# Strassen's scheme for the recurrence's values, and the token sums made earlier in the program, in a one-core hybrid decoder layer

## The chip, the cores and the metric

The kernel runs on one core of one Trainium2 chip. A core has a matmul engine (TensorE, PE in the profile, with its weight loads as PEld), an elementwise engine (VectorE, DVE), an activation engine (ScalarE, ACT), a general engine (GpSimd, POOL), a queue engine (SyncE, SP), and 16 DMA engines that serve the queues of SP, ACT and POOL. The metric is the device time of one execution in microseconds (us), as the median of several runs.

## What is computed

A decoder layer on x of 512 tokens by 1024 channels, float32. After an RMS norm, h goes through one wide matrix `w_in`; its columns are split into the inputs of two branches and of their gates. The first branch is a gated linear recurrence with 8 heads of 128 channels, the second a latent attention. What matters here is the first branch:

```
proj = h @ w_in[l]
hq, hf, hi, hz, cq, ckv, kr, mz, glog = split(proj)
f = lb + (1 - lb) * sigmoid(hf);  q = silu(hq);  k = 1 - f;  v = hi
o = hgrn2_recurrence(q, k, v, log(f))           # S_t = diag(f_t) S_{t-1} + k_t v_t^T,  o_t = S_t^T q_t
y_a = rms_norm(o, hg_norm_g) * silu(hz)
y_b = mla_branch(cq, ckv, kr, mz, ...)
gates = sigmoid(glog + b_gate)
x = x + (gates_a * (y_a @ w_proj_a) + gates_b * (y_b @ w_proj_b)) @ w_out
out = rms_norm(x, final_norm_g)
```

The values v are hi = h @ w_in[:, 2048:3072]: 512 x 1024 times 1024 x 1024.

## The kernel before

**Precision.** Every float32 matmul is made of three. Each operand is split into a high part (rounded to the matmul's format by ACT) and a low part (what is left, by DVE), and high x high, high x low and low x high are added up in PSUM. `mm3` (L99) issues the three for one k (a block of 128 channels). `load_w` (L110) fetches a weight piece of 128 x 1024 elements by SP's queue into one of three raw buffers, casts its high part on ACT (L129) and subtracts for the low part on DVE (L130); there are four buffers for high and four for low parts. `split` (L169) does the same for data that is in SBUF or PSUM already.

**Stages.** First x is normed and transposed into hT, which holds h as channels by tokens, high and low (to about 25 us). Then the latent projection (L398 to L403), its norms, and the transposes into cT (L425). Then the recurrence by pairs of heads, `hg_pair` (L585): the forget projection, `hg_forget` (the gates' running products on DVE and POOL), then for pairs 0 and 2 the values of four heads at once, the query projection, transposes, states, the gate projection, scores and outputs. For pairs 1 and 3 the gate projection stands where the values are. Then the attention heads, and last the two gates' projections, the two output projections and `w_out`.

**The values.** `proj_tok` (L151) makes 512 columns for all 512 tokens: two rounds of two token tiles of 128, eight k each, three matmuls of 128 x 512 each, 96 in all. Its four weight pieces stay in their buffers until the second round has used them. ACT copies each tile to SBUF (`v_sb`, L603). Pair 0 makes the columns of heads 0 to 3, pair 2 those of heads 4 to 7.

**Strassen's scheme elsewhere.** The gates' projections, `w_proj_a` and `w_out` are done already as seven products of half blocks instead of eight, in Winograd's form. They need four sums of blocks of h (s1 to s4) and four sums of blocks of the weight. The weight sums are made in DRAM: SP copies a block (`BlockSums.start`, one copy queued behind each weight load, L793), and POOL's queue adds another block by an accumulating DMA (`BlockSums.add`, L800). `step` (L845) issues one such sum at fixed places in the pairs and heads, from the list `adds`, behind the last POOL instruction traced. The sums of h are made by `early_sums` (L816) in two halves, one inside pair 0 and one behind it, and SP writes their high and low parts to DRAM (L830), from where POOL's queue fetches them before the gates (L1002).

**What orders the work.** Some blocks are marked as scheduled by hand for PE, ACT or DVE. Everything else is ordered before the run by the framework, engine by engine, from a model of durations: of the instructions that it holds for ready, the one traced first goes first. `tc.issue_after(x)` puts instructions behind x on x's engine. On the chip every engine takes its instructions in that fixed order and waits by semaphores; a queue's DMAs are issued in order too. A pool of tiles with one buffer per tag makes a new tile wait for the last reader of the old one.

Of the kernel before, what the change touches and what calls it, by code (L numbers as in the profile page):

```python
# [9 lines left out]
F32 = mybir.dt.float32  # L10
# [28 lines left out]
def hybrid_layer(ctx: ExitStack, tc: tile.TileContext, a):  # L39
# [67 lines left out]
    last_hi, last_lo = [None], [None]  # L107
    queued = []

    def load_w(*pieces, to=None):  # L110
# [4 lines left out]
        for src in pieces:  # L115
# [12 lines left out]
            o += n  # L128
        last_hi[0] = nc.scalar.copy(hi[:, :o], raw[:, :o])  # L129
# [51 lines left out]
    kpe = Pair(cpool.tile([P, 2, S], F32R, "kpe")[:])  # L181
    cw = Pool("cwork", "right")
# [23 lines left out]
    x_sb = [st.tile([P, D], F32, "x", bufs=NT) for _ in range(NT)]  # L206
# [50 lines left out]
    def squares(t):  # L257
        sq = st.tile([P, D], F32, "sq", bufs=2)
        nc.scalar.activation(sq[:], x_sb[t][:], AF.Square, accum_out=rss[t][:, 0:1])
        power(rss[t][:, 0:1], rss[t][:, 0:1], 1.0 / D, EPS, neg_half[:, 0:1])  # L260
# [17 lines left out]
    def c_product(t, kh, kind, ks=range(4)):  # L278
# [3 lines left out]
        for k in ks:  # L282
            nc.tensor.matmul(ps, hT[l][:, 4 * kh + k, t * P : t * P + P], c_hl[kh][r][:, k * 256 : k * 256 + 256],  # L283
                             start=kh == 0 and kind == 0 and k == 0, stop=kh == 1 and kind == FIN and k == 3)

# [7 lines left out]
    with tc.manual_schedule(engines={mybir.EngineType.PE, mybir.EngineType.Activation, mybir.EngineType.DVE}):  # L293
# [49 lines left out]
        for t in range(1, NT):  # L343
            if t + 2 < NT:
                squares(t + 2)
            for kh in range(2):
                lo[kh]()
# [49 lines left out]
    c_second += [load_c2(j) for j in range(2, 4)]  # L397
    for t in range(NT):  # L398
# [4 lines left out]
        nc.scalar.copy(c_sb[:, t, 256:704], ps[:, 0:448])  # L403
    css = cw.tile([P, 2, NT], F32, "css")
# [31 lines left out]
    ya = ypool.tile([P, H, S], F32, tag="ya", name="ya")  # L436
    ma_pool = Pool("mla_a", "right")
    qtab = ma_pool.tile([P, 2, S], F32, "qtab")
    nc.gpsimd.dma_start(qtab[:], a["c_qtab"])
# [144 lines left out]

    def hg_pair(pair, in_forget=None, in_query=None, before_gate=None, last=None):  # L585
# [3 lines left out]
        if pair:  # L589
            step()  # L590
        else:
            early_sums(kh[0])
# [7 lines left out]
        if pair % 2 == 0:  # L600
            for t in range(NT):
                v_sb[t] = hw.tile([P, 512], F32, f"v{t}")
            proj_tok(w_in, COL_I + cc, hT, lambda t, ps: nc.scalar.copy(v_sb[t][:], ps[:]))  # L603
# [166 lines left out]
    kh = [slice(0, 2), slice(2, 4)]  # L770
    half_t = [slice(0, 256), slice(256, 512)]
    blocks = lambda t: (t[:, 0:4, half_t[0]], t[:, 4:8, half_t[0]], t[:, 0:4, half_t[1]], t[:, 4:8, half_t[1]])
    TERMS = ((0, 0), (1, 1), (0, 1), (1, 0))

    def minus(out, x, y):
        nc.vector.tensor_tensor(out, x, y, op=ALU.subtract)

    def minus_minus(out, x, y):

        nc.vector.scalar_tensor_tensor(out, x, -1.0, y, op0=ALU.mult, op1=ALU.subtract)  # L780

# [32 lines left out]
    h_dram = [[dram.tile([P, 4, 256], F32, name=f"h{n}{i}") for i in range(2)] for n in range(1, 5)]  # L814

    def early_sums(q):  # L816

        E = lambda tag: ma_pool.tile([P, 2, 256], F32, tag)[:]
        h11, h12, h21, h22 = zip(*[[b[:, q] for b in blocks(t)] for t in hT])

        def whole(tag, hl):
            out = E(tag)
            nc.vector.tensor_tensor(out, hl[0].bitcast(F32), hl[1].bitcast(F32), op=ALU.add)
            return out

        def keep(n, tag, src):
            hl = Pair(ma_pool.tile([P, 2, 2, 256], F32R, tag)[:])
            split(*hl, src)
            for i in range(2):
                nc.sync.dma_start(h_dram[n - 1][i][:, q], hl[i].bitcast(F32))  # L830

        e22, e21, e11, e12 = whole("qr", h22), whole("qs", h21), whole("qh", h11), whole("p3", h12)
        minus(e22, e22, e21)
        keep(1, "qn", e22)
        minus_minus(e22, e22, e11)
        keep(2, "kn", e22)
# [423 lines left out]
```

## Time and profile before

| | before |
|---|---|
| median of 3 runs | 609.73 us (609.5 to 609.87) |
| the profiled execution | 609.93 us |
| its span in the trace | 607.7 us |
| DMA | 114.37 MB, 74543 packets, mean 188 GB/s |
| DVE's costliest group, `w_lo` L130 | x116, 138.3 us busy |
| ACT's costliest group, `w_hi` L129 | x116, 115.1 us busy |

How to read it: the span runs from the first to the last instruction; busy times are counted within it, and TensorE's matmuls overlap, so the duration of one record is longer than the distance to the next. The chain that ended last is followed back from the last instruction to what released it. A wait row names the waiting instruction, the releaser, the total, the number of times and the longest. A stage row gives each engine's busy time in the stretch, with the instructions in brackets, then the granted TensorE clock, the share of the DMA engines' time, and the rate. DMA rows give the number, the size of one and the median time from issue to landing.

### The profile page before, as it was taken

How to read it: one execution, taken by the hardware profiler on the slowest of the kernel's cores; microseconds unless marked ns; L12 is line 12 of the kernel's file. 1: busy time of each engine (PE TensorE's matmuls, PEld its weight loads, DVE VectorE, ACT ScalarE, POOL GpSimd, SP SyncE). 2: the span in 40 equal slices, each digit the busy share in tenths (PEclk: the TensorE clock that was granted, in tenths of full speed). 3: DMA queues.
4: the chain of work that ended last, by engine and by line, in shares of the span. 5: the costliest groups of instructions: out<-in, count | busy, mean ns of one | idle time of the engine just before them, and what ended most of it. 6: DMA issues, size and time to landing. Idle time of an engine off the chain costs nothing.

```text
span 607.7 us, 9766 instructions
## 1 busy us (share of the span) xinstructions
PE 598.3 (98%) x3670; PEld 524.8 (86%) x3670; DVE 436.6 (72%) x684; ACT 286.2 (47%) x533; POOL 146.4 (24%) x253
## 2 busy tenths in 40 slices
PE   8999999999999999999999999999999999999995
PEld 5998888888888888888888888899999999888884
DVE  7717989599764548959767776747757678567886
ACT  6555245333313342435646555438757854424452
POOL 3106322254350137414254530400000000000012
PEclk9999999999999999999999999999999999999998
DMA  7549479987969967573369575866665564695113
GB/s 257 177 138 345 154 218 369 320 220 171 237 151 275 220 185 147 125 172 90 57 163 169 148 152 126 237 243 198 189 184 178 195 195 160 200 347 183 61 35 139
DMA packets 74543, 114.37 MB, mean 188 GB/s; under 512 B 7512, under 2 KB 41726, under 8 KB 74496
## 3 DMA queue, kind: packets, MB, share of 16 engines
q1 hardware_dynamic: 65244, 89.95, 46.1%
q0 software_dynamic: 8336, 22.55, 19.9%
q10 hardware_dynamic: 916, 1.25, 0.6%
q8 instruction: 29, 0.48, 0.3%
q14 instruction: 18, 0.15, 0.1%
HBM read 105.34 MB, written 39.85 MB: 239 GB/s over the span
## 4 chain that ended last, share of the span: by engine, by line
PE 96%; ACT 1%; DMA 1%; DVE 0%; issue 0%; SPq 0%; POOLq 0%; POOL 0%; ACTq 0%
PE mm_ps L102 19%; PE mm_ps L104 19%; PE mm_ps L103 19%; PE ax_ps L898 16%; PE ax_ps L1096 5%; PE mm_ps L898 3%; PE mm_ps L283 2%; PE ax_ps L757 1%; PE ax_ps L731 1%; PE ax_ps L559 1%; PE mm_ps L1096 1%; PE ax_ps L561 1%; PE ax_ps L521 1%; DMA w_raw<-w_in 1%; PE ax_ps L104 1%; PE ax_ps L103 1%
## 5 line engine op out<-in xcount | busy, mean ns | idle before, releaser
L130 DVE TENSOR_TENSOR w_lo<-w_raw,w_hi 128x1024 fp32r<-128x1024 f32 (+3 forms) x116 | 138.3, 1205 | 68.3 <-ACT w_hi L129 65.4
L129 ACT CAST w_hi<-w_raw 128x1024 fp32r<-128x1024 f32 (+3 forms) x116 | 115.1, 1005 | 130.1 <-PE mm_ps L103 56.5
L102 PE MATMUL mm_ps<-hT,w_hi 128*128 128x512 f32 x320 | 125.8, 394 | 0.0
L103 PE MATMUL mm_ps<-hT,w_hi 128*128 128x512 f32 x320 | 125.3, 391 | 0.0
L104 PE MATMUL mm_ps<-hT,w_lo 128*128 128x512 f32 x320 | 125.2, 393 | 0.0
L104 PEld LDWEIGHTS mm_ps<-hT,w_lo 128*128 128x128 f32 x320 | 60.1, 188 | 12.3
L102 PEld LDWEIGHTS mm_ps<-hT,w_hi 128*128 128x128 f32 x320 | 60.2, 188 | 11.9
L103 PEld LDWEIGHTS mm_ps<-hT,w_hi 128*128 128x128 f32 x320 | 60.2, 188 | 11.9
L898 PE MATMUL ax_ps<-s,w_hi 128*128 128x256 f32 x384 | 54.2, 283 | 0.2 <-ACT w_hi L129 0.2
L898 PEld LDWEIGHTS ax_ps<-s,w_hi 128*128 128x128 f32 x384 | 49.6, 192 | 0.5 <-ACT w_hi L129 0.5
L1147 POOL TENSOR_SCALAR ssum<-ssum 128x1 f32<-128x1 f32 x3 | 0.9, 309 | 188.0 <-ACT sq L1134 188.0
L103 PE MATMUL mm_ps<-w_lo,hT 128*128 128x512 f32 (+1 forms) x96 | 36.6, 383 | 0.0
L104 PE MATMUL mm_ps<-w_hi,hT 128*128 128x512 f32 (+1 forms) x96 | 36.5, 382 | 0.0
L102 PE MATMUL mm_ps<-w_hi,hT 128*128 128x512 f32 (+1 forms) x96 | 36.2, 386 | 0.0
L739 ACT ACTIVATE p<-ax_ps,sm 128x128 f32<-128x128 f32 (+3 forms) x32 | 16.7, 525 | 35.4 <-DVE sm L738 32.8
L741 POOL TENSOR_SCALAR p<-p,sm 128x128 f32<-128x128 f32 (+3 forms) x28 | 15.6, 560 | 66.2 <-DVE sm L740 54.9
L898 PE MATMUL ax_ps<-s,w_lo 128*128 128x256 f32 x192 | 31.4, 284 | 0.0
L469 DVE RECIPROCAL tf<-pr 128x512 f32<-128x512 f32 x8 | 26.8, 3348 | 0.1
L898 PEld LDWEIGHTS ax_ps<-s,w_lo 128*128 128x128 f32 x192 | 26.6, 192 | 0.2 <-DVE w_lo L130 0.2
L102 PE MATMUL mm_ps<-cT,w_hi 128*128 128x512 f32 x52 | 20.7, 397 | 0.0
L104 PEld LDWEIGHTS mm_ps<-w_hi,hT 128*128 128x128 f32 x96 | 18.0, 188 | 3.0
L102 PEld LDWEIGHTS mm_ps<-w_hi,hT 128*128 128x128 f32 x96 | 18.0, 188 | 2.9
(308 smaller groups left out, 1204.8 us busy)
## 6 DMA issues: line engine op xcount, KB each, us to landing
w_raw<-w_in SPq DMA_DIRECT2D x54, 512.0 KB, 6.4
g_t<-w_in SPq DMA_DIRECT2D x16, 512.0 KB, 9.1
w_raw<-g_t SPq DMA_DIRECT2D x16, 512.0 KB, 4.4
g_t<-w_in POOLq DMA_DIRECT2D x8, 512.0 KB, 10.5
pa_t<-w_proj_a SPq DMA_DIRECT2D x8, 512.0 KB, 8.9
g_t<-g_t POOLq DMA_DIRECT2D x8, 512.0 KB, 9.5
out_t<-w_out SPq DMA_DIRECT2D x8, 512.0 KB, 8.0
s<-h POOLq DMA_DIRECT2D x8, 512.0 KB, 11.6
```

The costliest lines, as they stand in the source:

```text
L102: nc.tensor.matmul(ps, lh[lsl], rh[rsl], start=start, stop=False)
L103: nc.tensor.matmul(ps, lh[lsl], rl[rsl], start=False, stop=False)
L104: nc.tensor.matmul(ps, ll[lsl], rh[rsl], start=False, stop=stop)
L129: last_hi[0] = nc.scalar.copy(hi[:, :o], raw[:, :o])
L130: last_lo[0] = nc.vector.tensor_tensor(lo[:, :o], raw[:, :o], hi[:, :o].bitcast(F32), op=ALU.subtract)
L283: nc.tensor.matmul(ps, hT[l][:, 4 * kh + k, t * P : t * P + P], c_hl[kh][r][:, k * 256 : k * 256 + 256], start=kh == 0 and kind == 0 and k ...
L469: nc.vector.reciprocal(rp[:], pr[:])
L521: nc.tensor.matmul(sps[:, sl], kt_[:, sl], v_sb[i][:, (h % 4) * P : (h % 4) * P + P], start=True, stop=True)
L739: last_act[0] = nc.scalar.activation(p[:, :n], sps[:, :n], AF.Exp, scale=SCALE, bias=sm[:, 1:2], accum_out=sm[:, 2:3])
L741: scaled_p = (nc.vector if final else nc.gpsimd).tensor_scalar(p[:, :n], p[:, :n], sm[:, 3:4], 0.5, op0=ALU.mult, op1=ALU.mult)
L898: nc.tensor.matmul(ps[:, o], w[k // 2][i][:, k % 2, cols], ap[j][:, k], start=not banks and c == 0 and n == 0, stop=n == 11, skip_group_ch ...
L1096: nc.tensor.matmul(ps[:, o : o + n], ap[i][:, k, t * P : t * P + P], w[k // 2][j][:, k % 2, o : o + n], start=fresh and c == 0, stop=c == ...
```

## The change

The values are computed as one product of 512 x 1024 by 1024 x 1024 in Winograd's form of Strassen's scheme, with blocks of 256 tokens x 512 channels and of 512 channels x 512 columns. Seven products of 24 matmuls take the place of the two `proj_tok` of 96. Five of them run in pair 0 (`values_first`): h11 with w00, s2 with the sum of three weight blocks, s3 with the sum of two, h12 with w10, and h22 with the sum of four. They give heads 0 to 3, and four tiles (`v_late`) that wait in SBUF for pair 2. There the other two run (`values_rest`): s1 with w00 + w01, and s4 with w11, for heads 4 to 7.

What comes with it: `early_sums` is traced once, behind the latent projection and before its norms, on whole blocks, and keeps s2 and s3 in SBUF for the first pair; all four sums go to DRAM by POOL's queue. The first and the last of them share two staging tiles. The weight sums are made in SBUF, in the tile `ya`, which also holds x at the start: SP loads blocks, POOL's queue adds one by two accumulating DMAs, DVE adds the others. Behind pair 0 `fetch_rest` loads a block of the weight and s1 and s4 again by SP (six DMAs of 512 KB), and `RestSum` adds a block to the former by POOL's queue at pair 1's first step. Pair 0 now issues a sum at its first step too, so that the list with its one entry more is at the same place from pair 1's second step on. The rope table `qtab` shares a tile with the sums and is loaded behind pair 2.

```diff
+    ya = ypool.tile([P, H, S], F32, tag="ya", name="ya")
+    ma_pool = Pool("mla_a", "right")
...
-    x_sb = [st.tile([P, D], F32, "x", bufs=NT) for _ in range(NT)]
+    x_sb = [ya[:, 2 * t : 2 * t + 2].rearrange("p k c -> p (k c)") for t in range(NT)]
...
+    i_w3, i_w2 = ya[:, 0:4], ya[:, 4:8]
+    KEEP = {1: ("qn", "kn"), 2: ("qn", "kn"), 3: ("qp", "qtab"), 4: ("qp", "qtab")}
+    def early_sums():
+        es = Pool("early", "left")
...
+        def keep(n, src):
+            hls = kept(n) if n in (2, 3) else [Pair(es.tile([P, 2, 2, 256], F32R, f"s{i}")[:]) for i in range(2)]
+            for q, hl in zip(kh, hls):
+                split(*hl, src[:, q])
+                nc.gpsimd.dma_start(h_dram[n - 1][:, :, q], hl.both.bitcast(F32))
+            return hls
+        e22, e21, e11 = whole("e22", h22), whole("e21", h21), whole("e11", h11)
+        minus(e22, e22, e21)
+        keep(1, e22)
+        minus_minus(e22, e22, e11)
+        s2 = keep(2, e22)
+        minus(e21, e11, e21)
+        s3 = keep(3, e21)
+        e12 = whole("e12", h12)
+        minus_minus(e12, e12, e22)
+        keep(4, e12)
...
     c_second += [load_c2(j) for j in range(2, 4)]
+    c_lo_last = last_lo[0]
+    for q in kh:
+        nc.sync.dma_start(i_w3[:, q], i_w[0, 1][:, q])
+    for q in kh:
+        nc.gpsimd.dma_start(i_w3[:, q], i_w[1, 1][:, q], accum_op=ALU.add)
+    for q in kh:
+        nc.sync.dma_start(i_w2[:, q], i_w[0, 0][:, q])
...
+    with tc.issue_after(c_lo_last.ins):
+        s_kept = early_sums()
+        for q in kh:
+            nc.vector.tensor_tensor(i_w2[:, q], i_w2[:, q], i_w3[:, q], op=ALU.add)
...
+    def v_product(ap, w, done, banks=None, tile=ax_tile):
+        res = banks or [tile() for _ in range(2)]
+        for t, ps in enumerate(res):
+            for n, (x, k) in enumerate((x, k) for x in range(3) for k in range(4)):
+                i, j = ((0, 0), (1, 0), (0, 1))[x]
+                nc.tensor.matmul(ps[:], ap(i, k, t), w[k // 2][j][:, k % 2], start=not banks and n == 0, stop=n == 11,
+                                 skip_group_check=banks is not None)
+            done(t, ps)
+        return res
...
+        u = v_product(h11, i_block(0, 0), lambda t, ps: nc.scalar.copy(v_sb[t][:], ps[:]))
+        v_product(s2, i_split(i_w2), late(2), u)
+        v_product(s3, i_split(i_w3), late(3), u)
+        w10, raws = [], []
+        for q in kh:
+            w10.append(load_w(i_w[1, 0][:, q]))
+            nc.vector.tensor_tensor(i_w2[:, q], i_w2[:, q], last_raw[0].rearrange("p (k c) -> p k c", k=2), op=ALU.add)
+        v_product(h12, w10, lambda t, ps: nc.vector.tensor_tensor(v_sb[t][:], v_sb[t][:], ps[:], op=ALU.add), tile=mm_tile)
+        v_product(h22, i_split(i_w2), lambda t, ps: nc.scalar.copy(v_sb[2 + t][:], ps[:]), u)
...
+        r = v_product(of_sum(s_late[1]), i_split(i_w2), rest(3), tile=mm_tile)
+        v_product(of_sum(s_late[4]), i_block(1, 1), rest(2), r)
...
-        if pair:
-            step()
-        else:
-            early_sums(kh[0])
+        step()
...
-            proj_tok(w_in, COL_I + cc, hT, lambda t, ps: nc.scalar.copy(v_sb[t][:], ps[:]))
+            (values_rest if pair else values_first)()
...
-                nc.sync.dma_start(h_dram[n - 1][i][:, q], hl[i].bitcast(F32))
...
         if pair == 0:
-            early_sums(kh[1])
+            with tc.issue_after(last_dma[0].ins):
+                fetch_rest()
     early = []
+    qtab = ma_pool.tile([P, 2, S], F32, "qtab")
+    nc.gpsimd.dma_start(qtab[:], a["c_qtab"])
```

`late(n)` copies the negated sum of a product tile to `v_late` on ACT; `rest(n)` subtracts a tile from `v_late` into `v_sb` on DVE; `i_split` splits a weight sum that is in SBUF.

More of the change, by code (lines that the diff above doesn't have):

```diff
@@ L107, in hybrid_layer @@
     last_hi, last_lo = [None], [None]
+    last_raw = [None]
     queued = []
@@ L128, in load_w @@
             o += n
+        last_raw[0] = raw[:, :o]
         last_hi[0] = nc.scalar.copy(hi[:, :o], raw[:, :o])
@@ L345, in hybrid_layer @@
                 squares(t + 2)
-            for kh in range(2):
-                lo[kh]()
+            for n in range(2):
+                lo[n]()
             if t + 1 < NT:
@@ new lines, in i_block, with i_split, values_first, late @@
+    def i_block(i, j):
+        return [load_w(i_w[i, j][:, q]) for q in kh]
+    def i_split(raw):
+        res = []
+        for q in kh:
+            hi, lo = [pool.tile([P, WCH], F32R, tag=tag, name=f"w_{tag}")[:].rearrange("p (k c) -> p k c", k=2)
+                      for pool, tag in ((whi, "hi"), (wlo, "lo"))]
+            split(hi, lo, raw[:, q])
+            res.append((hi, lo))
+        return res
+    v_late = {}
+    def values_first():
+        h11, h12, h21, h22 = [of_block(hl) for hl in zip(*[blocks(t) for t in hT])]
+        s2, s3 = [of_sum(s) for s in s_kept]
+        def late(n):
+            def done(t, ps):
+                v_late[n, t] = ma_pool.tile([P, S], F32, ("qr", "qs", "qh", "p3")[2 * (n - 2) + t])
+                nc.scalar.activation(v_late[n, t][:], ps[:], AF.Copy, scale=-1.0)
+            return done
+        u = v_product(h11, i_block(0, 0), lambda t, ps: nc.scalar.copy(v_sb[t][:], ps[:]))
+        v_product(s2, i_split(i_w2), late(2), u)
+        v_product(s3, i_split(i_w3), late(3), u)
+        w10, raws = [], []
+        for q in kh:
+            w10.append(load_w(i_w[1, 0][:, q]))
+            nc.vector.tensor_tensor(i_w2[:, q], i_w2[:, q], last_raw[0].rearrange("p (k c) -> p k c", k=2), op=ALU.add)
+        v_product(h12, w10, lambda t, ps: nc.vector.tensor_tensor(v_sb[t][:], v_sb[t][:], ps[:], op=ALU.add), tile=mm_tile)
+        v_product(h22, i_split(i_w2), lambda t, ps: nc.scalar.copy(v_sb[2 + t][:], ps[:]), u)
@@ new lines, in hybrid_layer, with add, fetch_rest @@
+    s_late = {}
+    class RestSum:
+        def add(self):
+            with tc.issue_after(last_pool[0].ins):
+                for q in kh:
+                    nc.gpsimd.dma_start(i_w2[:, q], i_w[0, 1][:, q], accum_op=ALU.add)
+    def fetch_rest():
+        for q in kh:
+            nc.sync.dma_start(i_w2[:, q], i_w[0, 0][:, q])
+        for n in (1, 4):
+            s_late[n] = kept(n)
+            for q, hl in zip(kh, s_late[n]):
+                nc.sync.dma_start(hl.both.bitcast(F32), h_dram[n - 1][:, :, q])
@@ L813, in hybrid_layer @@
     out_w = BlockSums("out", a["w_out"][0])
[L814 to L829, printed above, removed]
-                nc.sync.dma_start(h_dram[n - 1][i][:, q], hl[i].bitcast(F32))
[L832 to L836, printed above, removed]
-        minus(e21, e11, e21)
-        keep(3, "qp", e21)
-        minus_minus(e12, e12, e22)
-        keep(4, "qn", e12)
-    adds = [(gate_w[0], 0), (gate_w[0], 2), (gate_w[1], 0), (gate_w[0], 1), (gate_w[1], 2), (gate_w[0], 3), (gate_w[1], 1),
+    adds = [(gate_w[0], 0), (gate_w[0], 2), (gate_w[1], 0), (RestSum(),), (gate_w[0], 1), (gate_w[1], 2), (gate_w[0], 3), (gate_w[1], 1),
             (pa_w, 0), (gate_w[1], 3), (pa_w, 2), None, (pa_w, 1), (out_w, 0), (pa_w, 3), (out_w, 2), (out_w, 1), (out_w, 3)]
```

47 lines of the change are left out of this document (32 added, 15 removed).

## The prediction, made before the changed kernel was run

> **What bounds the kernel now.** I read the page's busy times first, then TensorE's waits, then the chain that ended last, and last the engines by stage. The profiled execution took 609.93 us, 2.23 us more than its span; the median of the three runs is 609.73 us, 0.20 us below it.
>
> ```profile
> span 607.7 us, 9766 instructions
> PE 598.3 (98%) x3670; PEld 524.8 (86%) x3670; DVE 436.6 (72%) x684; ACT 286.2 (47%) x533; POOL 146.4 (24%) x253
> ...
> PE 96%; ACT 1%; DMA 1%; DVE 0%; issue 0%; SPq 0%; POOLq 0%; POOL 0%; ACTq 0%
> ```
>
> PE (TensorE) is busy for 598.3 of 607.7 us and makes 96% of the chain that ended last. Its waits by releaser, with total, count and longest, are only these four:
>
> ```profile
> PE ax_ps L248 <- DVE zero L294: 1.2, 1, 1.2
> PE mm_ps L283 <- ACT hT L274: 0.6, 1, 0.6
> PE ax_ps L898 <- ACT w_hi L129: 0.2, 1, 0.2
> PE ax_ps L272 <- DVE xn L264: 0.2, 1, 0.2
> ```
>
> None of them is in a projection, in the recurrence or in its values. Through those stages PE never stands still, so its work is the time, and whatever else is done there is hidden until it makes PE wait.
>
> A busy share says nothing about the price of one matmul, because matmuls overlap. The price is the distance between starts. Two matmuls of the old values in the third pair, and two whole products of the new kind in the last stage (24 matmuls of 128x512 with three terms and four k), show it (start, us, what):
>
> ```profile
> 175.33 0.39 PE L103 MATMUL mm_ps<-w_lo,hT 128*128 128x512 f32 x1
> ...
> 182.59 0.39 PE L104 MATMUL mm_ps<-w_hi,hT 128*128 128x512 f32 x1
> ```
> ```profile
> 562.41 5.44 PE ax_ps L1096 x24
> 567.86 5.44 PE mm_ps L1096 x24
> ```
>
> Between the first two starts lie 32 steps: 7.26 / 32 = 0.227 us for a matmul whose record says 0.39. One product is 5.44 / 24 = 0.227 us a matmul, the same. Old form and new form cost PE alike for each matmul; only the count changes.
>
> **The matmuls.** Each of the two old value projections has 4 token tiles x 8 k x 3 terms = 96 matmuls, together 192. Seven products of 24 are 168. So 24 fall away: 24 x 0.227 = 5.44 us. They don't fall evenly. The first pair goes from 96 to 120 (+5.44 us on PE), the third pair from 96 to 48 (-10.88 us). Nothing else is added to PE: the sums go to VectorE (DVE) and to accumulating DMAs.
>
> **DVE and ScalarE (ACT).** The prices, start to start, from these rows:
>
> ```profile
> 42.97 3.50 DVE L130 TENSOR_TENSOR w_lo<-w_raw,w_hi 128x1024 fp32r<-128x1024 f32 x3 [12.19 <-ACT w_hi L129]
> ...
> 65.55 0.69 DVE L823 TENSOR_TENSOR qr<-hT,hT 128x512 f32<-128x512 f32 x1
> 66.15 0.69 DVE L823 TENSOR_TENSOR qs<-hT,hT 128x512 f32<-128x512 f32 x1
> ...
> 105.04 0.68 DVE L581 SCALAR_TENSOR_TENSOR z<-z,mm_ps 128x512 f32<-128x512 f32 x1
> ```
> ```profile
> 41.91 2.00 ACT L129 CAST w_hi<-w_raw 128x1024 fp32r<-128x1024 f32 x2
> ```
> ```profile
> L603 ACT COPY v<-mm_ps x8: 581/586/587, 69.1 to 186.2; 128x512 f32<-128x512 f32 x8
> ```
>
> DVE takes 3.50 / 3 = 1.17 us for 1024 elements and 0.60 us for 512; ACT 1.0 us for a cast of 1024, 0.59 us for a copy from PSUM.
>
> The token sums were 2 x (8 sums + 4 splits' lower parts) at 0.60 = 14.4 us of DVE, in and behind the first pair. They become 8 x 1.17 + 8 x 0.60 = 14.2 us, queued on DVE right behind the last split of the latent projection's weights. Their 8 casts on ACT move along.
>
> The values of the first pair need ten weight splits on DVE instead of four, four sums of weights and two additions from PSUM (0.68 us each): 14 x 1.17 + 2 x 0.68 = 17.8 us against 4.7, so +13.1. On ACT come six casts and four copies more, 6 x 1.0 + 4 x 0.59 = 8.4 us. In the third pair the splits stay four, DVE gets four more operations on PSUM (2.7 us), and ACT loses four copies.
>
> By stage, PE, PEld, DVE, ACT, POOL busy (instructions), clock, DMA share, GB/s:
>
> ```profile
> 15.20:30.40 15.20, 14.94 (x107) 14.04 (x106) 11.05 (x24) 8.55 (x14) 2.30 (x7) 1.00 0.53 177
> 30.40:45.60 15.20, 15.20 (x77) 14.04 (x76) 2.98 (x7) 7.93 (x19) 0.00 (x0) 1.00 0.42 138
> 45.60:60.80 15.20, 15.20 (x79) 12.87 (x78) 10.88 (x15) 7.88 (x14) 9.60 (x21) 1.00 1.03 346
> 60.80:76.00 15.20, 15.20 (x71) 12.57 (x70) 15.20 (x20) 4.03 (x7) 5.89 (x12) 1.00 0.43 153
> ```
> ```profile
> 66.00:107.00 41.00, 41.00 (x257) 34.10 (x256) 38.64 (x54) 17.54 (x26) 14.14 (x17) 1.00 0.82 266
> 160.00:230.00 70.00, 70.00 (x422) 59.19 (x421) 41.60 (x49) 24.02 (x57) 22.14 (x43) 1.00 0.86 212
> ```
>
> The sums leave a stretch in which DVE is full (15.20 of 15.20, 38.64 of 41.00) and go to one in which it has 15.20 - 2.98 = 12.2 us free, with 4.3 free just after (15.20 - 10.88). There 14.2 us fit, with 2.3 us of the weights' first sum behind them. The first pair trades 14.4 us of DVE for 13.1 and gets 5.44 us more of PE to hide it under. The third pair loses 10.88 us of cover, and DVE has 70 - 41.6 = 28.4 us free there, ACT 46. So I cost all of DVE and ACT at nothing; the matmuls beside them are the cover. If it is gone, the price is what runs over: 14.2 + 2.3 - 12.2 - 4.3 = 0, so nothing to a microsecond.
>
> **Queues.** The sums' writes to DRAM move from SP (16 of 256 KB) to POOL's queue (8 of 512 KB), behind two accumulating DMAs for a weight sum; SP gets four value loads ahead of the latent stage's end. These rows price them:
>
> ```profile
> 45.90 1.17 POOL L414 TENSOR_TENSOR kd<-c_sb,ktab 128x256 f32<-128x256 f32 x1 [27.84 <-ACT c_sb L403]
> ```
> ```profile
> 28.03 0.39 SPq L123 DMA_DIRECT2D w_raw<-w_in  x1
> ...
> 30.39 0.38 SPq L123 DMA_DIRECT2D w_raw<-w_in  x1
> ...
> 44.23 0.38 SPq L123 DMA_DIRECT2D w_raw<-w_in  x1
> ```
> ```profile
> g_t<-w_in POOLq DMA_DIRECT2D x8, 512.0 KB, 10.5
> ...
> s<-h POOLq DMA_DIRECT2D x8, 512.0 KB, 11.6
> ...
> h<-qn SPq DMA_DIRECT2D x8, 256.0 KB, 4.5
> ```
>
> POOL stood idle for 27.84 us before 45.90, so ten issues there delay no other work of POOL if they are done by then. On SP, all three buffers for raw weights are refilled by 30.39 and the next load goes out at 44.23; ACT casts the first of them at 41.91. That is some 12 us of slack for four more loads. The reload behind the first pair (six of 512 KB on SP, ahead of the second pair's loads) has the first pair's own prefetch as cover. The accumulation for the third pair comes one step early in the second pair on POOL and lands in some 10.5 us, a whole pair ahead of its use. The other weight sums keep their step from there on, since the first pair now has one step more. The rope table's DMA moves behind the third pair, ahead of its use in the fourth. The inputs' move into the recurrence's output tile changes no transfer. Waits are added at two places: DVE's first weight sum waits for the accumulation (10.5 us), and behind it stand the weight splits of the first pair; and the last token sum reuses the staging tiles of the first, so that ACT and DVE wait for a write on POOL's queue. No trace shows these two waits; their bounds are nothing and, for each, a PE stop as rivals A and B price it. They can't bring a gain, since PE has no waits there to lose. I take 0.2 us, the row of PE's one wait for weights.
>
> **Sum.** 609.73 - 5.44 + 0.2 = 604.5 us (604.7 for a profile like this one). With its own small errors (0.2 us of spread of runs, matmuls somewhat dearer behind transposes, a microsecond of stops) this case gives 603.7 to 605.6.
>
> **Rivals.**
>
> A: DMA becomes the bound before the values. Between 15.20 and 60.80 the rows moved (177 + 138 + 346) GB/s x 15.2 us = 10.05 MB. The change puts 14 transfers of 512 KB there (four loads, two accumulations, eight writes), 7.34 MB. At 346 GB/s, with the share at 1.03 the most these rows show, 17.39 MB take 50.3 us instead of 45.6, so 4.7 us late. If PE waited for all of it, the gain is nearly gone: 609.73 - 5.44 + 4.7 = 609.0 us; half of it gives 606.6. For it: the writes on POOL's queue interleave with SP's loads. Against it: the stretch behind is at 153 GB/s, the loads PE needs first go out before the writes, and prefetches for later stages can be late at no cost. The Trainium skill (Trainium Kernel Development and Optimization, Key Constraints) says that DMAs from the SP, ACT and POOL queues run on the same 16 engines and interleave, so another queue saves only issue time. By it the move to POOL's queue takes no bytes out of the loads' way, which is this rival; no run here shows that yet.
>
> B, slower: ACT stops behind the staging tiles. In the run before, the same kind of wait is this row (total, count, longest):
>
> ```profile
> ACT qn L171 <- DMA h<-qn: 4.6, 2, 3.7
> ```
>
> Its writes landed in 4.5 us; POOL's 512 KB need 11.6. That makes the wait 3.7 + 7.1 = 10.8 us. If the cast that waits stands ahead of the forget weights' two casts (41.91 us), these end at 41.91 + 10.8 + 2.0 = 54.7, and PE, which starts on those weights at 45.25, stands for 9.5 us:
>
> ```profile
> 45.25 0.23 PE mm_ps L102
> ```
>
> The time would be 609.73 - 5.44 + 9.5 = 613.8 us. It decides against the change from 5.44 + 1.2 = 6.7 us of stop on. Against it: instructions on an engine are ordered before the run by expected readiness, and the weights' casts are ready first.
>
> C: the third pair doesn't shrink. The gain there is 10.88 us, the loss in the first pair 5.44. If the forget and query chains on DVE and not PE set the third pair's length, the loss remains: 609.73 + 5.44 = 615.2 us at worst, and from less than half the shrinkage on the change doesn't pay. Against it: DVE is at 41.60 of 70 us there. For it: the old values stood between forget and query and gave that chain 21.8 us of cover, which becomes 10.9.
>
> **How the numbers follow.** Forecast 0.70, A 0.14, B 0.09, C 0.07. A measurement of this kernel tells about 0.2% (1.2 us) from no change, so faster means below 608.5. The forecast is faster throughout, of A 0.11 are and 0.03 are no change; of B 0.02 and of C 0.02 come out level, the rest slower. That gives 0.81 faster, 0.07 same, 0.12 slower. The range runs from the forecast's low end, 603.7, to 608.5 in rival A, and leaves out a little under 2 in 10.
>
> **What would show it.** Right: 24 fewer matmuls (about 3646, a few records can be missing), PE's busy time 5.4 us less, no PE wait above a microsecond between 25 and 110 us, the matmul of the values still at 0.227 us from start to start; DVE over 12 us busy between 30 and 46; the third pair 10.9 us shorter, the first 5.4 longer. Wrong: a PE wait on a weight cast or split near 45 us (B, with ACT idle before it for a DMA from the sums' writes; A, with ACT waiting for raw weights), or PE idle in the third pair behind DVE's chain (C). Were the matmul count unchanged, or the products' matmuls dearer than 0.227 us, the sum itself would be wrong.

## The result, and the profile after

| | before | after |
|---|---|---|
| median | 609.73 us (609.5 to 610.45, 5 runs) | 629.26 us (627.78 to 631.78, 5 runs) |
| the profiled execution | 609.93 us | 627.78 us |
| its span | 607.7 us | 626.0 us |
| TensorE (PE) idle in the span | 9.4 us | 25.6 us |

The change made the kernel slower: ratio 1.0327, 95% interval 1.031 to 1.0343. The forecast was 604.5 us, with a range from 603.7 to 608.5. In this table and below, a run over 1.5% above the fastest of its kernel counts in the median but not in the ratio; that is one run each of chain_and_spread and late_sums_held_b. The page of the kernel after:

```profile
span 626.0 us, 9746 instructions
PE 600.4 (96%) x3646; PEld 523.5 (84%) x3646; DVE 455.1 (73%) x692; ACT 291.7 (47%) x539; POOL 156.4 (25%) x265
...
PEclk9998899979999999999999999999999999999999
...
PE 74%; DMA 12%; DVE 6%; ACT 3%; issue 2%; POOL 2%; SPq 0%; POOLq 0%; ACTq 0%; DVEq 0%
```

The 24 matmuls are gone (3646 for 3670), yet PE is busy for 2.1 us longer, its granted clock dips at two places, and the chain that ended last has 12% of DMA in place of 1%. The span grew by 18.3 us, and that divides into three terms. The matmuls took off 5.44. PE idles 25.6 - 9.4 = 16.2 longer. And its busy time is 600.4 - (598.3 - 5.44) = 7.5 longer than the matmuls that are left should need. Who makes PE wait (total, count, longest; the four largest rows):

```profile
PE mm_ps L102 <- DVE z L644: 7.8, 2, 6.0
PE ax_ps L492 <- DVE c_sb L488: 5.1, 2, 4.3
PE ax_ps L660 <- ACT v L690: 1.7, 1, 1.7
PE ax_ps L638 <- DVE k L630: 1.7, 1, 1.7
```

DVE and ACT are named. But behind the first two rows the chain of waits goes on to three weight loads (start, us from issue to landing):

```profile
29.93 21.11 DMA w_raw<-w_in
...
115.27 14.59 DMA w_raw<-w_in
...
210.75 21.97 DMA w_raw<-w_in
```

Each stands behind one stop: at 55 to 67 us, at 127 to 133, and at 234 to 237. The two rows of 1.7 us, at 75 and 196 us, have no load next to them in the chain; what stands ahead of them there is other work of ACT and DVE. The first stop, step by step over the engines (the timeline; in brackets the idle time before a row, and who ended it):

```profile
51.12 1.05 ACT L131 CAST w_hi<-w_raw 128x1024 fp32r<-128x1024 f32 x1 [6.63 <-DMA w_raw<-w_in]
52.07 0.53 ACT L466 COPY c_sb<-mm_ps 128x448 f32<-128x448 f32 x1
...
52.68 1.34 POOL L481 TENSOR_TENSOR kd<-c_sb,ktab 128x256 f32<-128x256 f32 x1 [7.18 <-ACT c_sb L466]
...
58.99 5.04 DVE L488 TENSOR_SCALAR c_sb<-c_sb,css 128x384 f32<-128x384 f32 x8 [2.17 <-POOL css L179]
...
59.47 3.31 PE L492 MATMUL ax_ps<-ident,c_sb 128*128 128x128 f32 x13 [4.29 <-DVE c_sb L488]
```

Read it from the top. ACT waits 6.63 us for a value weight that nothing needs yet. Behind that cast, in ACT's fixed order, stands the last copy of the latent projection, whose data has long been ready: at 52.07, where it ran at 45.28 before. POOL's norm waits for that copy, DVE's scaling for POOL, and PE's transposes for DVE. A late load has stopped a chain that does not use it.

The stages at that place (rows as in the prediction) show the cause of the lateness:

```profile
30.40:45.60 15.20, 15.20 (x77) 13.76 (x75) 15.01 (x21) 9.46 (x23) 5.54 (x7) 1.00 1.08 310
45.60:60.80 15.20, 10.91 (x47) 8.47 (x47) 7.51 (x10) 5.52 (x10) 7.87 (x10) 0.90 1.04 377
60.80:76.00 15.20, 12.30 (x50) 9.54 (x50) 15.20 (x18) 8.48 (x12) 3.67 (x8) 0.77 0.47 170
```

From 30 to 46 us the DMA engines went from a share of 0.42 and 138 GB/s to 1.08 and 310; they are full up to 61. DVE is 15.01 of 15.20 us busy in the first row, as forecast.

Of the 7.5 us of longer busy time some 5 are the clock. Its column in stretches of 4 us, and the distance of the matmuls' starts behind the second stop:

```profile
56.00:60.00 4.00, 0.53 (x2) 0.39 (x3) 1.83 (x5) 1.99 (x2) 3.75 (x7) 0.71 1.04 369
60.00:64.00 4.00, 3.21 (x14) 2.41 (x13) 4.00 (x7) 2.02 (x3) 3.37 (x9) 0.50 0.98 390
64.00:68.00 4.00, 3.59 (x15) 2.72 (x15) 4.00 (x6) 2.43 (x3) 0.00 (x0) 0.51 0.55 165
...
130.00:134.00 4.00, 1.08 (x3) 0.89 (x4) 2.81 (x4) 3.04 (x4) 0.00 (x0) 0.50 1.02 359
134.00:138.00 4.00, 4.00 (x17) 3.26 (x16) 3.10 (x5) 0.76 (x1) 0.00 (x0) 0.73 1.03 345
```
```profile
133.94 0.63 PE L104 MATMUL mm_ps<-hT,w_lo 128*128 128x512 f32 x1
134.36 0.63 PE L102 MATMUL mm_ps<-hT,w_hi 128*128 128x512 f32 x1
...
136.58 0.39 PE L102 MATMUL mm_ps<-hT,w_hi 128*128 128x512 f32 x1
136.81 0.39 PE L103 MATMUL mm_ps<-hT,w_hi 128*128 128x512 f32 x1
```

After these two stops the granted clock is 0.50, and a matmul takes 0.42 us from start to start where 0.23 is normal. PE's busy time in a row, times what its clock lacks to 1.00, is 0.2 + 1.6 + 1.8 + 0.5 + 1.1 = 5.1 us over the five rows. The other 2.4 us are not explained by the clock. The first stop (4.29, 0.79 and 0.41 us) and the second (5.97) are 11.5 us together, so they are paid for about one and a half times: (11.5 + 5.1) / 11.5. The full clock is back some 3 us after PE's restart at the second stop, and some 8 us after it at the first, where PE stood twice more. The Trainium skill (TensorE: Matmul & The Clock Gate, The HAM clock gate) has this as a rule: half rate after an idle window of some 3.4 us, full rate after as long a busy one. The second stop agrees with it, in its 5.97 us and in the return (132.92 to 136.35); other stops of these runs do not, as the last section shows.

### The profile page after: what moved, and what is told of

Its sections match the earlier page's. It is cut to its first block, busy times and chain, and to the rows that moved or that the text cites. A ratio compares the mean times of both kernels' runs of the same rounds, so it can differ in the third digit from the quotient of the medians.

```text
span 626.0 us, 9746 instructions
## 1 busy us (share of the span) xinstructions
PE 600.4 (96%) x3646; PEld 523.5 (84%) x3646; DVE 455.1 (73%) x692; ACT 291.7 (47%) x539; POOL 156.4 (25%) x265
## 2 busy tenths in 40 slices
DMA packets 76655, 120.65 MB, mean 193 GB/s; under 512 B 7576, under 2 KB 41790, under 8 KB 76608
## 4 chain that ended last, share of the span: by engine, by line
PE 74%; DMA 12%; DVE 6%; ACT 3%; issue 2%; POOL 2%; SPq 0%; POOLq 0%; ACTq 0%; DVEq 0%
PE ax_ps L1002 16%; DMA w_raw<-w_in 11%; PE mm_ps L102 10%; PE mm_ps L104 10%; PE mm_ps L103 10%; PE ax_ps L1200 5%; PE ax_ps L660 3%; PE mm_ps L1002 3%; PE mm_ps L660 3%; DVE w_lo L132 2%; PE mm_ps L287 2%; PE ax_ps L897 1%; PE ax_ps L871 1%; ACT w_hi L131 1%; PE ax_ps L622 1%
## 5 line engine op out<-in xcount | busy, mean ns | idle before, releaser
L132 DVE TENSOR_TENSOR w_lo<-w_raw,w_hi 128x1024 fp32r<-128x1024 f32 (+3 forms) x114 | 135.5, 1201 | 74.5 <-ACT w_hi L131 72.9
L131 ACT CAST w_hi<-w_raw 128x1024 fp32r<-128x1024 f32 (+3 forms) x114 | 112.8, 1004 | 139.5 <-PE mm_ps L103 52.9
L529 POOL TENSOR_SCALAR k<-tf,c1n,c 128x512 f32<-128x512 f32 x8 | 14.2, 1778 | 26.0 <-ACT tf L526 26.0
L102 PE MATMUL mm_ps<-cT,w_hi 128*128 128x512 f32 x52 | 20.6, 397 | 0.0
L104 PE MATMUL mm_ps<-cT,w_lo 128*128 128x512 f32 x52 | 20.4, 393 | 0.0
L103 PE MATMUL mm_ps<-cT,w_hi 128*128 128x512 f32 x52 | 20.4, 391 | 0.0
L1002 PE MATMUL ax_ps<-hT,w_hi 128*128 128x256 f32 x128 | 18.0, 283 | 0.0
L1002 PEld LDWEIGHTS ax_ps<-hT,w_hi 128*128 128x128 f32 x128 | 16.5, 192 | 0.0
## 6 DMA issues: line engine op xcount, KB each, us to landing
s<-h POOLq DMA_DIRECT2D x8, 512.0 KB, 10.9
```

What stands on the lines that cost most here:

```text
L102: nc.tensor.matmul(ps, lh[lsl], rh[rsl], start=start, stop=False)
L103: nc.tensor.matmul(ps, lh[lsl], rl[rsl], start=False, stop=False)
L104: nc.tensor.matmul(ps, ll[lsl], rh[rsl], start=False, stop=stop)
L132: last_lo[0] = nc.vector.tensor_tensor(lo[:, :o], raw[:, :o], hi[:, :o].bitcast(F32), op=ALU.subtract)
L529: nc.gpsimd.tensor_scalar(k[:], tf[:], c1n[:, h : h + 1], c1[:, h : h + 1], op0=ALU.mult, op1=ALU.add)
L1002: nc.tensor.matmul(ps[:, o], w[k // 2][i][:, k % 2, cols], ap[j][:, k], start=not banks and c == 0 and n == 0, stop=n == 11, skip_group_ch ...
```

## The experiments

Theory L: loads land late, and in-order queues carry the lateness to work that does not need them. Rival V: it is the volume itself, so that something waits whatever the order. Rival D: the added DVE and ACT work sets the time. All ratios are to before on the same chip.

**cast_behind.** On ACT the late value weight's cast stands behind the last of the latent's squares; nothing else.

```diff
+            last_csq = nc.scalar.activation(csq[:, :n], ...)
...
-        u = v_product(h11, i_block(0, 0), ...)
+        with tc.issue_after(last_csq.ins):
+            w00 = i_block(0, 0)
+        u = v_product(h11, w00, ...)
```

> Theory L (late loads): the third weight load of the first pair took 21.1 us to land, its cast on ACT stood ahead of the last latent copy, and so ACT held up the norm, the transposes and PE; PE then ran at half clock. With only that cast moved behind the copies and squares, the first stop of PE (7 us idle between 45 and 76 us and some 4 us of slow clock) goes: about 618 us against 629. Rival D (DVE): the token sums and weight sums on DVE hold the scaling of the latent tile, whatever ACT does; then this edit changes little: 626 to 630.

624.58 us, ratio 1.0238 (1.0217 to 1.0258): 4.7 us better than the change, less than L expected. The copy moved up to 44.83 us, but then this stood ahead of the scaling on DVE (timeline):

```profile
52.98 1.23 DVE L132 TENSOR_TENSOR w_lo<-w_raw,w_hi 128x1024 fp32r<-128x1024 f32 x1 [5.18 <-ACT w_hi L131]
...
55.33 4.51 DVE L488 TENSOR_SCALAR c_sb<-c_sb,css 128x384 f32<-128x384 f32 x8
```

The same late weight, its low part now: the block has moved from ACT's queue to DVE's. PE's stop there fell from 5.1 to 2.6 us, but the granted clock behind it fell to 0.50 all the same, from 58 to 64 us.

**spread_fetch** and **cast_and_spread.** The six reloads behind the first pair go out one by one, each behind a weight load of the second pair, in place of the block copies there, which all come six loads later. In both kernels one gate weight sum is made before its copy arrives, so that they do not compute that sum; their matmuls (3646) and bytes (120.65 MB) are those of the change. The second has the edit of cast_behind too.

```diff
     def fetch_rest():
-        for q in kh:
-            nc.sync.dma_start(i_w2[:, q], i_w[0, 0][:, q])
...
+        late_loads = [lambda q=q: nc.sync.dma_start(i_w2[:, q], i_w[0, 0][:, q]) for q in kh]
...
+        queued[0:0] = late_loads
```

> Only the six reloads behind the first pair are changed: instead of six in a row on SP's queue, one goes out behind each of the six weight loads of the second pair. Theory L: the load that took 14.6 us at 115 lands in 6 to 8, the 6 us stop of PE at 127 to 133 and its 2 us of slow clock go: about 621 us; the first stop stays. Rival P (the longer first pair or the shorter third pair itself, not the transfers): no change, 627 to 631.

> Both edits together. Theory L: the two stops are separate, so the gains add: 609 to 612 us; what is left above 604.5 is the stops in the third pair (4 us). Rivals D and P: above 622 us.

624.39 us, 1.0246 (1.0231 to 1.0262), and 621.87 us, 1.0191 (1.0151 to 1.0231). In spread_fetch the stop at 127 us is gone. But a new one of 3.7 us stands at 288 us, where ACT stood 7.50 us in issuing three swaps of the attention's rope. Together the edits gave 7.4 us where 17 to 20 were expected, since stops moved on.

**sums_loads_last.** The four block loads, the two accumulations and DVE's additions for the weight sums come behind the first value load.

```diff
+        w00 = [load_w(i_w[0, 0][:, kh[0]])]
+        with tc.issue_after(last_dma[0].ins):
+            for q in kh:
+                nc.sync.dma_start(i_w3[:, q], i_w[0, 1][:, q])
...
```

> The four loads for the weight sums and their accumulations are put behind the third weight load on SP's queue, nothing else. If the place in SP's queue made that load late (theory L in its narrow form), it lands within 12 us instead of 21 and the first stop goes: about 618 us. If the whole volume of DMA in the stretch made it late, wherever a load stands in the queue, it lands after some 18 us or more and the time stays above 624.

625.92 us, 1.0254 (1.0224 to 1.0283). The third weight load, now ahead of the four block loads, landed in 6.5 us, as the narrow form of theory L has it; the gain of 11 us that was to follow did not come. PE's stop before the transposes went from 5.1 to 2.0 us, with a new one of 2.1 us next to it: DVE's addition of the sum, which needs an accumulation that took 12.9 us to land, now stood ahead of the scaling. Moving the same bytes back only changed which transfer was late.

**volume_later.** Four writes of token sums and four block copies, 4 MB, leave the stretch before 51 us, and the first pair's weight sums start one step later.

```diff
+                if n in (1, 4):
+                    nc.gpsimd.dma_start(h_dram[n - 1][:, :, q], hl.both.bitcast(F32))
...
+        with tc.issue_after(last_dma[0].ins):
+            for n, s in ((2, s_kept[0]), (3, s_kept[1])):
+                for q, hl in zip(kh, s):
+                    nc.sync.dma_start(h_dram[n - 1][:, :, q], hl.both.bitcast(F32))
...
+    queued, burst = [], [0, 0, 0, 0, 2, 2, 2, 2]
```

> Only transfers move: the writes of s2 and s3 to DRAM (four of 512 KB) go out by SP behind the value weights instead of by POOL's queue at 39 to 45 us, and the four block copies behind the first four loads of the first pair go out with the next four; the first pair's weight sums start one step later. No instruction of ACT or DVE moves. If the volume in the stretch from 25 to 51 us is what made the load issued at 29.93 us land 21 us later, 4 MB of some 9.4 MB are gone from it, the load lands in about 12 us, ACT's wait in front of the latent copy (6.6 us) goes, and with it the first stop of TensorE (some 6 us, and 3.5 us of half clock behind it): 620 us. If the order on SP's own queue sets the landing, whatever else runs, it lands in 18 us or more and the time stays at 627 to 630. A stop of 6 us at 130 us should stay in both cases.

629.2 us, 1.0325 (1.0307 to 1.0344): no gain at all, and still the volume theory was right about the landing. The weight loads from 24 to 56 us (the answer for their line), and the stages:

```profile
DMA to landing us min/median/max: 7.5/10.0/11.7
```
```profile
44.00:48.00 4.00, 3.60 (x17) 2.71 (x16) 4.00 (x4) 3.88 (x9) 2.00 (x3) 1.00 0.16 26
48.00:52.00 4.00, 4.00 (x20) 3.30 (x19) 4.00 (x5) 2.06 (x2) 3.83 (x4) 1.00 0.59 180
52.00:56.00 4.00, 4.00 (x19) 3.34 (x18) 4.00 (x7) 0.00 (x0) 3.85 (x6) 1.00 1.06 323
```

The loads land within 12 us instead of 21, and the DMA engines are nearly idle at 44 to 48 us. But DVE is full in every row. The scaling starts at 53.50 us (50.44 in the kernel before), when POOL's norm has been ready for 0.8 us only: POOL took from 46.00 to 52.74 for the rope and that norm, where before needed from 45.90 to 50.44. Why POOL was slower beside the full DVE was not tried. The larger part of the stop comes behind the scaling, from what stands on DVE ahead of the low parts of cT (PE's wait, then DVE's timeline):

```profile
PE ax_ps L500 <- DVE cT L496: 2.5, 1, 2.5
```
```profile
59.14 1.21 DVE L698 TENSOR_TENSOR ya<-ya,w_raw 128x1024 f32<-128x1024 f32 x1
60.28 1.21 DVE L175 TENSOR_TENSOR w_lo<-ya,w_hi 128x1024 fp32r<-128x1024 f32 x1
```

With the loads in time the additions and splits for the products, ready sooner, stood ahead of the latent's chain by right. So rival D has its part here: two causes lay one on the other, and the expectation was wrong in that the framework's order on ACT and DVE did change with the transfers.

**chain_first.** The late weight's cast and low part, the last token sum's splits and both additions stand behind the latent's squares (ACT) and its scaling (DVE). No transfer moves.

```diff
+            last_scale = nc.vector.tensor_scalar(c_sb[:, t, o : o + n], ...)
+    with tc.issue_after(last_csq.ins), tc.issue_after(last_scale.ins):
+        keep_s4()
+        for q in kh:
+            nc.vector.tensor_tensor(i_w2[:, q], i_w2[:, q], i_w3[:, q], op=ALU.add)
...
+        with tc.issue_after(last_csq.ins), tc.issue_after(last_scale.ins):
+            w00 = i_block(0, 0)
```

> Only the order on ACT and DVE moves: the late value weight's cast and its low-part split, the last token sum's casts and splits and both additions of the weight sum stand behind the squares (ACT) and behind the scaling of the latent (DVE). No transfer moves; the load still lands 21 us after its issue. If the two in-order queues are what turns the late load into a stop, the first stop shrinks to the 1 to 2 us by which the products themselves have to wait, with no half clock behind it: 620 us. If the products, whose weight is as late as ever, then wait for the same time, the time is that of the run in which only the cast moved: 624 to 625.

620.74 us, 1.0187 (1.016 to 1.0215), as theory L said. The first stop is down to 0.59 us. Order alone, with the loads as late as ever, gave 8.5 us. A third of 3.0 us, at 238 us, stands behind a swap that ACT's queue issued when a block copy had landed, 19.56 us after its issue. The second stop remains, with its late load (waits, then chain):

```profile
PE mm_ps L102 <- ACT w_hi L131: 3.0, 1, 3.0
```
```profile
95.77 22.05 DMA w_raw<-w_in
```

**chain_and_spread** and **all_three.** The former is chain_first with the spread reloads and the list of weight sums in an order that fits. The latter has volume_later's transfers as well.

```diff
+    adds = [..., (RestSum(),), (gate_w[0], 1), (gate_w[0], 3), (gate_w[1], 1), (gate_w[1], 2), ...]
```

> The order of chain_first, and the six reloads behind the first pair go out one by one in the place of the block copies of the second pair (with the list of weight sums put in an order that fits). If the first two stops are two separate cases of late loads in front of in-order engines, both go: 629.3 - 9 - 8 = 612. If stops only move on, 617 or more.

> The order of chain_first, the spread reloads, and the transfers of volume_later. If the queues and the volume are the whole loss, 604.7 and a few us of small stops in later stages remain: 606 to 609, faster than before. If the third pair or a later stage has a loss of its own from the change, 611 or more.

617.73 us, 1.0116 (1.0072 to 1.0161), and 618.56 us, 1.0146 (1.0127 to 1.0166): both above what theory L expected. In chain_and_spread the first two stops are gone or under 1 us; all_three still has one of 2.1 us at 60 us, behind DVE. Taking volume away on top gave nothing. What remains of chain_and_spread is this (timeline; ACTq is ACT's queue of DMA issues):

```profile
267.44 7.56 ACTq L789 DMA_DIRECT2D qs<-qr  x3
...
279.69 0.79 PE L102 MATMUL ax_ps<-kn,qn 128*128 128x512 f32 x1 [3.72 <-DVE k L630]
```

ACT stands 7.56 us in issuing three swaps of the attention's rope, and the outputs' norms behind them come late. The block copies that the reloads had pushed back were in their way.

**held_copies.** The last four copies go out some 35 us later.

```diff
+        queued[-4:-4] = [lambda: None] * 6
```

> Chain_and_spread with one edit: the last four block copies of w_out, which its spread reloads had pushed to 249 to 260 us, next to the four small swaps of the first attention head's rope (ACT's queue stood for 7.56 us there), go out some 35 us later instead. If these copies in front of the swaps are what makes the stop of 3.7 us at 280 us, it goes, with its half clock (1.6 us): 617.7 - 5 = 612 to 613. If the stop there comes from the accumulating sums, which keep their place, the time stays at 616 to 618.

611.23 us, 1.0038 (1.0021 to 1.0054): a little better than expected, and the stop at 280 us is gone. Four copies moved by 35 us made the difference between ratios of 1.0116 and 1.0038: 4.8 us, or 2 to 8 with the widths of both intervals.

**best_order.** Four more copies go out in the first pair; two more groups of casts move back on ACT.

```diff
+    queued, burst = [], [1] * 6 + [2] * 4
...
+        with tc.issue_after(v_copy[-1].ins):
+            w3 = i_split(i_w3)
...
+        with tc.issue_after(last_act[0].ins):
+            w2 = i_split(i_w2)
```

> The order of chain_first and spread reloads; four more block copies with the last four loads of the first pair, where the DMA engines stand idle, so that only two are late, and these two held back behind the swaps; the casts of the second weight sum behind the copies of the first products' values on ACT, and those of the third pair's sum behind the turned keys' copy. If late transfers in front of in-order queues are the whole loss, every stop over 1 us is gone, and the time is the predicted sum with some 2 us of small stops: 605 to 608, faster than before. If DVE or PE have a further loss in the stages that the change rebuilt, 610 or more.

613.38 us, 1.0073 (1.0053 to 1.0094): a miss. The stops that the casts' edit was meant for are gone. With the added copies came a new one of 2.9 us at 108 us, where the reloads go.

**late_sums_held** and **late_sums_held_b.** Held_copies with the casts' edit of best_order, and the copies in a list of their own (`None` is a load with no copy; numbers count them).

```diff
+        rest, none = list(queued), lambda: None
+        queued[:] = late_loads + [none if e is None else rest[e - 10] for e in (10, ..., 17,
+            20, 21, None, None, None, None, 18, 19, 24, 25, 22, None, None, None, None, 23, 28, 29, 26, 27, 30, 31)]
```

> Held_copies without its two kinds of stop that are left. First, four block copies no longer go out beside the fourth pair's loads at 193 to 215 us (there a load took 18 us, and ACT waited for it 5.3 and 4.8 us in front of the swaps and the outputs' squares), but later, among the attention heads. Second, the casts of the second weight sum stand behind the copies of the first products' values on ACT, and those of the third pair's sum behind the turned keys' copy. The stops of 1.29, 0.48, 1.11 and 0.76 us go, and 1.7 us of half clock behind them: 611.2 - 5.3 = 606, faster than before by 0.5%, if late transfers in front of in-order queues are the whole loss. If the stretch is slow for a reason of the third pair's own (less PE work beside the same chain), the stop at 227 us stays: 609 to 610.

> The same with one of those four copies left beside the fourth pair's loads, and the last of the others 10 us sooner, ahead of the swaps. If each copy there costs its share, some 0.5 to 1 us slower than the other; if not, the same 606.

612.05 us, 1.0026 (1.0004 to 1.0047), and 611.67 us, 1.0036 (1.0012 to 1.0061): not the 606 expected. Their runs spread from 607.98 to 615.74 us and from 608.99 to 617.08, where before has 609.1 to 610.59. In the profiled runs stops of 0.8 and 2.3 us stand at 217 and 220 us, at the end of the third pair, behind a gate projection whose weights landed late.

**sums_in_attention** and **sums_and_latent.** The sums of w_proj_a and their copies move out of the third and fourth pairs; the second also puts the late weight behind the latent's last transpose on ACT and DVE.

```diff
+    adds = [..., (gate_w[1], 1), None, (gate_w[1], 2),
+            None, (gate_w[1], 3), None, (pa_w, 0), (pa_w, 2, 1), (out_w, 0), (pa_w, 3), (out_w, 2, 1), (out_w, 3)]
...
+        with tc.issue_after(ct_hi.ins), tc.issue_after(ct_lo.ins):
+            w00 = [load_w(i_w[0, 0][:, kh[0]])]
```

> Late_sums_held, with the sums of w_proj_a and their eight block copies (16 MB of traffic with reading and writing) moved from the third and fourth pairs to the attention heads, where the DMA engines are busy for half of the time. If the loads' 20 us in 190 to 220 us are the volume beside them, they land in under 12 us, the stops of 0.76 to 2.3 us at 217 to 220 us go, and the runs lie closer together: 607 to 609. If the third pair is too short for its own loads, whatever runs beside them, 611 to 612 as before.

> The same, and ACT casts the late value weight behind the latent's last transpose copy, DVE splits it behind the last of its subtractions there, with the two additions of the weight sum behind that. The stop of 1.8 us at 59.7 us (transposes that wait for DVE) goes: 605 to 607, and faster than before by over 0.2%. If the products then wait for the weight's low part, as late as ever, the gain is under 0.5 us.

618.48 us, 1.0153 (1.0125 to 1.0181), and 615.48 us, 1.0092 (1.008 to 1.0104): two misses. The stop at 217 us is gone in both and the one at 60 us in the second, as expected, but one of 5 us stands in the attention. In sums_and_latent (timeline, then chain):

```profile
348.56 0.48 PE L908 MATMUL ax_ps<-ident,p 128*128 128x128 f32 x1 [5.38 <-POOL p L892]
```
```profile
325.65 21.09 DMA w_raw<-w_ukv
```

Six accumulating transfers had gone out at 319 to 327 us, and the load issued in their midst landed 21 us later. Meanwhile ACT stood 14.60 us in issuing four swaps of the rope, where before needs 2.44 at that place; what PE waited for stood behind them in ACT's order. It is the stop of chain_and_spread again at another place.

**sums_spread** and **latent_order_held.** The former is sums_and_latent with one sum at the fourth pair's last step and the others one by one. The latter is late_sums_held with the latent's order alone.

```diff
+            None, (gate_w[1], 3), (pa_w, 0), (pa_w, 2), (pa_w, 1), (out_w, 0), (pa_w, 3), (out_w, 2, 1), (out_w, 3)]
```

> Sums_and_latent with one sum of w_proj_a at the fourth pair's last step and the others one by one at the heads' steps, and the copies of w_out thinned out behind 300 us. The stop of 5.4 us at 349 us goes, and the half clock behind it (some 4 us in 340 to 360): 615.5 - 9.5 = 606, faster than before by 0.6%, if late transfers are the whole loss. If the volume is too much for the stages wherever it is put, a stop of 3 to 5 us stands elsewhere and the time stays over 610.

> Late_sums_held with the latent's order of sums_and_latent and nothing else. Its stop of 1.8 us at 59.7 us goes: 610, as wide from run to run as there (608 to 615), since the third pair's sums and copies stay where they were.

Sums_spread takes 606.85 us (605.47 to 608.5), ratio 0.995 (0.9936 to 0.9964): faster than before by half a percent, with the same matmuls, sums and bytes (120.65 MB) as the change. Its page and its waits, all over 0.3 us:

```profile
span 605.4 us, 9747 instructions
...
PE 594.5 (98%) x3646; PEld 520.4 (86%) x3646; DVE 450.9 (74%) x692; ACT 290.6 (48%) x539; POOL 163.3 (27%) x265
```
```profile
PE ax_ps L252 <- DVE zero L348: 1.2, 1, 1.2
PE mm_ps L658 <- DVE v L731: 1.0, 1, 1.0
PE ax_ps L908 <- POOL p L892: 0.7, 1, 0.7
PE ax_ps L658 <- ACT w_hi L131: 0.6, 1, 0.6
```

Latent_order_held stayed at 611.21 us, 1.0016 (1.0 to 1.0032): its stop at 60 us went, one of 2.6 us at 217 us stayed, about as expected (610). What is shown by sums_spread is that the whole 22 us between 629.26 and 606.85 lay in the order of transfers and of the instructions behind them. Rival V is refuted by it, and of rival D what blames the amount of work, since both amounts are those of the change. How much of the 22 us was late loads, and how much work of DVE and ACT that stood ahead of something urgent without a late load, no run separates.

## Why the prediction was wrong

**The matmuls: right.** 24 fewer, at 0.227 us with the full clock. The sum came true only where the order was mended: PE's busy time in sums_spread is 594.5, 1.6 us above 598.3 - 5.44, and it idles 10.9 us against 9.4. These 3.1 us, less the 0.2 that was allowed and 0.4 by which the time outside the span is shorter, are the 2.6 us that the forecast for a profile, 604.7, misses there (607.25). One reading ahead of the sum doesn't stand, at no cost to it: of the four waits of before two are in projections after all (L283 is the latent's first columns, L898 one of the later Strassen products), 0.8 us together.

**Queues: the step that failed.** "That is some 12 us of slack for four more loads" counted SP's idle time between two issues. But a load's slack is what its reader has, and a busy engine's queue is not free because its issuer is idle. SP had been waiting for a buffer; the DMA engines then had to move the loads, the copy behind each weight load, the accumulations and the writes together, and a load that had taken 6.0 us (the median of seven from 26 to 60 us) took 21. That the reload "has the first pair's own prefetch as cover" failed in the same way at 115.27 (14.6 us). In place of the 0.2 us taken stand 16.2 us of stops, most of them behind three late loads, some 5 us of half clock, and 2.4 us of busy time without a known cause.

**DVE and ACT "at nothing": wrong as well, but hidden.** The 14.2 us went into the 12.2 free, as the row of 15.01 us shows. The sum of reserves was zero ("so nothing to a microsecond"), and nothing was charged for what stands behind that work in DVE's order. In the change the late load covered this; volume_later laid it bare.

**The rivals.** A had the place and the cause right and the price wrong. It charged the excess volume once, 4.7 us, as if PE waited for the last byte. In fact one 512 KB load came 21 us after its issue, ACT and DVE carried that to the latent chain, and the same happened at two more weight loads. The sentence from the Trainium skill there (Trainium Kernel Development and Optimization, Key Constraints: queues of several engines share 16 DMA engines and interleave) is borne out by the rows of 1.04 to 1.08, and by volume_later, where SP's loads landed sooner with half of POOL's writes and four of SP's copies gone from beside them; it spoke for A more strongly than the 0.14 it got. B did not happen: ACT's casts for the reused staging tiles waited for no write in the change. (In sums_loads_last one did, 3.43 us, beside a longer wait of DVE for the accumulation.) What B pictured, a wait at the head of an in-order engine, did happen, with loads as its cause. C is refuted. The gates' first step of the third pair and of the fourth (before, then sums_spread):

```profile
157.69 0.60 ACT L463 ACTIVATE tf<-mm_ps 128x512 f32<-128x512 f32 x1 [6.29 <-PE mm_ps L104]
...
226.47 0.60 ACT L463 ACTIVATE tf<-mm_ps 128x512 f32<-128x512 f32 x1 [1.89 <-PE mm_ps L104]
```
```profile
164.22 0.60 ACT L524 ACTIVATE tf<-mm_ps 128x512 f32<-128x512 f32 x1 [1.92 <-PE mm_ps L104]
...
223.96 0.60 ACT L524 ACTIVATE tf<-mm_ps 128x512 f32<-128x512 f32 x1 [1.89 <-PE mm_ps L104]
```

The third pair takes 59.7 us instead of 68.8, 9.0 of the 10.9 forecast. But the same loads then come in less time, which is probably why it was the hardest place to mend.

**The range.** It had no term for a stop's second price, the clock, nor for more than one stop at a time.

Open: why single runs of the kernels with late loads differ by up to 8 us, while those of before and of sums_spread keep within 1.5 and 3. A good part of it is the clock: in late_sums_held_b it goes from 0.999 in the run of 608.99 us to 0.988 in that of 617.08. What makes it differ is open, and so is what the last 1.6 us of PE's busy time in sums_spread are, and the 2.4 in the change.

## What to carry to other kernels

When a change adds transfers to a stretch, don't ask whether the issuing queue is idle: add up all bytes in flight there, take the landing time from a row with a full DMA share, and look on each engine at what stands behind the instruction that reads the load. A prefetch that comes late is harmless only if its cast stands behind everything urgent in the engine's order; putting it there gave 8.5 us without moving a byte. And where PE is the bound, expect to pay more than a stop's own length, since the clock may fall behind it: about one and a half times here for the first two stops, and about twice for the one of 2.97 us in chain_first (4 us rows from 116 to 128).

## What the hardware showed beside

The clock also fell behind a stop of 2.97 us, in chain_first, where starts are 0.43 us apart up to 124.7, and behind shorter ones: 2.57 us in latent_order_held at 217 us, 2.34 in late_sums_held_b at 220. Those are shorter than the Trainium skill's 3.4 us, and here the measurement decides. No length decides by itself: the same stop at 59.7 us left the clock at 1.00 in late_sums_held (1.78 us) and halved it in late_sums_held_b (1.71 us, 0.50 from 62 to 64). In the change the stops of 1.70 and 1.86 us left it at 1.00. What else decides was not tried.

DVE's eight scalings of the latent took 5.04 us in the change and 2.61 in chain_and_spread, where POOL stood idle from 51.5 us on (the timeline of the change, then that of chain_and_spread):

```profile
58.99 5.04 DVE L488 TENSOR_SCALAR c_sb<-c_sb,css 128x384 f32<-128x384 f32 x8 [2.17 <-POOL css L179]
...
60.29 1.47 POOL L326 DMA_DIRECT2D h<-s  x2
61.53 0.77 POOL L505 MEMSET fr<- 128x512 f32 x1
```
```profile
50.19 2.61 DVE L484 TENSOR_SCALAR c_sb<-c_sb,css 128x384 f32<-128x384 f32 x8 [3.84 <-POOL css L179]
```

That POOL's work beside it is the cause was not tried by itself.
